# State-space decay without selecting products: exponents loaded onto all partitions, all differences by ScalarE; the residual's loads two pieces ahead

## The chip, the core and the metric

The kernel runs on one core of a Trainium2 chip. The metric is the device time of one execution in microseconds (us), from the first to the last instruction with what lies around them; lower is better. The core has TensorE (PE: matrix products, with PEld for its weight loads), VectorE (DVE), ScalarE (ACT), GpSimd (POOL) and SyncE (SP, which here only issues transfers). The engines run their own instruction streams in order and wait for each other through semaphores. PSUM is the memory into which TensorE writes; SBUF holds the operands.

## The reference

One inference step of a one-layer decoder: attention over a sliding window beside a state-space mixer (Mamba-2 SSD), whose outputs are concatenated, projected (`w_out`) and added to the residual, then a squared-ReLU MLP. There are 1040 prompt tokens (16 meta tokens and 1024) and 32 sample tokens (8 sequences of 4). What matters here is the chunked scan: 8 heads of 64, 2 groups, a state of 128, chunks of 128 tokens.

```python
def ssd_scan(x, dt, a, bm, cm, h0, chunk):
    ...
    xdt = (x * dt[..., None]).reshape(b, nc, chunk, H, P)
    acum = jnp.cumsum((dt * a).reshape(b, nc, chunk, H), axis=2)
    causal = jnp.tril(jnp.ones((chunk, chunk), dtype=bool))[None, None, :, :, None]
    seg = acum[:, :, :, None, :] - acum[:, :, None, :, :]
    decay = jnp.exp(jnp.where(causal, seg, -jnp.inf))
    g = jnp.einsum('bcthn,bcshn->bctsh', ch, bh) * decay
    y_diag = jnp.einsum('bctsh,bcshp->bcthp', g, xdt)
    to_end = jnp.exp(acum[:, :, -1:, :] - acum)
    s_chunk = jnp.einsum('bclhn,bclh,bclhp->bchpn', bh, to_end, xdt)
    total = jnp.exp(acum[:, :, -1, :])
    ...
    y_off = jnp.einsum('bclhn,bchpn->bclhp', ch, h_in) * jnp.exp(acum)[..., None]
    return (y_diag + y_off).reshape(b, L, H, P), h_final
```

`decay` is the object of the change: for each head a matrix of exp(acum[t] - acum[s]) for s up to t. So is exp(acum[t]), the factor of `y_off`.

## The kernel before

Tokens lie along the free dimension and features along the partitions, in 9 token tiles: tile 0 holds the 32 sample tokens and the 16 meta tokens (48), tiles 1 to 8 hold 128 each. Products with weights run in three token chunks of 304 or 288, 384 and 384 columns, and each value is split in two parts (`hi`, `lo`), so that a product is three matmuls per block of 128 features (`gemm`).

The work goes through these parts: the input projections with the attention and the convolution between them (`projections`, up to about 291 us of the profile), then `wout_stream`, then the MLP from about 448 us on.

`wout_stream` goes over the output projection twice. First 24 pieces (8 row blocks times 3 chunks) with the attention half of `w_out`: for each piece it loads the residual `hb` from `xm`, runs a `gemm` of 12 matmuls into a PSUM tile `g`, adds `g` to `hb` on VectorE (L1007) and stores `hb` to `hd` in device memory (L1008). Then, once the state-space output is there, pieces with the other half (`mixer_half`), which read `hd` back into `ha` and store to `he`.

Between the first 24 pieces `interleave` weaves the chains of the state-space tiles: a chain is a Python generator, a slot is one piece with one step of each live chain before it, and a chain starts at its slot. This sets the order in which the program is written down; the planner of the tile framework then sorts each engine's stream by its own costs and due times and lets a transfer move ahead of others where its buffer is free, so the order on SP and on the engines is near the program's, not equal to it. In the trace the first three residual loads stand on SP ahead of the first store of a piece. A tile with a tag and `bufs=n` has n buffers, and the instruction that first writes the n+1st waits until the oldest is no longer read.

The decay before the change. At about 108 us `steps` has the cumulated sums `acum` per token (partition) and head, and writes `A4` with 32 columns per tile: the sum split in two parts (`Ah` and the rest), and the same negated. In the later stage `exponents` (called for tile 0, and for tiles 1 to 4 and 5 to 8 together) turns `A4` by a transpose into a PSUM tile and builds three operands: `L` (one side of the difference, per tile 32 rows), `R` (the other side, times a 0/1 pattern `delta` that picks the head) and `Tr` (the exponents in rows, for `selr`, a 0/1 pattern loaded from the constants). In `ssd(i)`, one product of `L` and `R` per group of four heads gives acum[t] - acum[s] for 4 heads at once in a PSUM tile `pd`; ScalarE takes Relu of the negated difference (L1085) and Exp of its negative (L1086) into `Mt`, and VectorE multiplies by `Gm`, the masked product of B and C (L1087). Four products of `selr` and `Tr` put acum[t] of the right heads onto the right partitions (`pe`), and ScalarE's Exp (L1092) makes `eA` of them.

The rest of `ssd(i)` is not touched: transposes of X and B into `px` and `pb` (L1060, L1062), `xd`, `xw`, `Bt`, `Gm`, the products `y` with `Mt`, the state `hn` and its product `f`, the products with `eA` (L1119) and the sums into X (L1122), then `gate(i)`. Tile 0 goes on with `sample_state` for the states of the sample sequences, which are loaded, scaled (L1183), added to and stored. PSUM tiles with the tag `s` have 3 buffers; `px`, `pb`, the two `pd`, `pe` and others share them.

## Time and profile before

| | |
|---|---|
| median of 3 runs | 1121.79 us (1121.38 to 1121.83) |
| the profiled execution | 1122.73 us |
| its span, first to last instruction | 1120.9 us |
| granted clock of TensorE | 0.999 of full speed |
| instructions | 21721 |

The profile is of one execution. Busy times are given per engine; a matmul's end is modelled and matmuls overlap, so a busy TensorE is not one at its peak, and the distance from one start to the next tells more than a duration. A row of the timeline is start, duration, engine, line and operation, output and inputs, shapes, and how many such instructions stand in it. A row of the waits is engine and line, what it waited for, microseconds in total, times, and the longest. Lines (L1085) are those of the kernel before. Most matmuls have the line of a helper, L205, and are told apart by their tiles.

### The profile page before, as it was taken

What the parts mean: (1) busy time and instruction counts of PE and PEld (TensorE: products, weight loads), DVE (VectorE), ACT (ScalarE), POOL (GpSimd) and SP (SyncE); (2) the same over time, 40 slices, a digit from 0 to 9 for tenths busy, and PEclk for the clock granted to TensorE, in tenths of its full rate; (3) what the DMA queues carried; (4) which work ended last, traced back from release to release, by engine and by line L of the source; (5) the groups of instructions that cost most, each with busy time, mean ns of one, the idle gap of its engine ahead of it and who ended that gap; (6) DMA issues with size and microseconds to landing.
All of it is one profiled execution on the core that took longest, in us unless ns stands there. A gap on an engine that the chain in (4) does not pass through costs nothing.

```text
span 1120.9 us, 21721 instructions
## 1 busy us (share of the span) xinstructions
PE 1105.1 (99%) x8347; PEld 1066.6 (95%) x8347; DVE 834.2 (74%) x1652; ACT 563.9 (50%) x1205; POOL 215.8 (19%) x298
## 2 busy tenths in 40 slices
PE   8999999999999999999999999999999999999997
PEld 8989988988888899999999999999999999999997
DVE  6646888985788968998877777676598657767483
ACT  7312467575766658754444444444434343546461
POOL 0442365564254431200000000000000000000001
PEclk9999999999999999999999999999999999999999
DMA  8231110111575486567643524425989663465273
GB/s 280 77 98 39 39 38 20 39 58 55 183 210 179 136 289 215 199 204 228 195 154 140 177 106 157 161 102 204 393 289 304 191 181 90 134 189 164 77 229 110
DMA packets 84423, 177.56 MB, mean 158 GB/s; under 512 B 10692, under 2 KB 32740, under 8 KB 82272
## 3 DMA queue, kind: packets, MB, share of 16 engines
q1 hardware_dynamic: 77392, 141.52, 40.6%
q0 software_dynamic: 6224, 33.74, 7.5%
q8 instruction: 65, 1.06, 0.4%
q10 hardware_dynamic: 704, 0.92, 0.2%
q14 instruction: 38, 0.31, 0.1%
HBM read 125.42 MB, written 50.72 MB: 157 GB/s over the span
## 4 chain that ended last, share of the span: by engine, by line
PE 77%; DVE 10%; ACT 5%; DMA 4%; issue 2%; POOL 2%; POOLq 0%; SPq 0%; ACTq 0%; DVEq 0%
PE g L205 42%; PE b L205 18%; PE c L205 9%; PE s L205 3%; DMA wdr<-in_wd 2%; PE o L205 1%; DVE bc L527 1%; DMA wraw<-in_win 1%; PE y L205 1%; POOL wlo L237 1%; DVE ts L1637 1%; DVE Sd L1623 1%; PE pt L205 1%; DVE p L680 1%; PE f L205 1%
## 5 line engine op out<-in xcount | busy, mean ns | idle before, releaser
L205 PE MATMUL g<-acth,whi 128*128 128x384 f32 (+2 forms) x528 | 161.8, 331 | 0.2 <-DVE qT L457 0.2
L205 PE MATMUL g<-acth,wlo 128*128 128x384 f32 (+2 forms) x528 | 159.2, 326 | 0.2 <-DVE hb L1007 0.2
L205 PE MATMUL g<-actl,whi 128*128 128x384 f32 (+2 forms) x432 | 140.5, 325 | 0.0
L1636 ACT CAST ts<-tr 128x528 fp32r<-128x528 f32 x92 | 58.2, 632 | 121.4 <-PE b L205 101.9
L1637 DVE TENSOR_TENSOR ts<-tr,ts 128x528 fp32r<-128x528 f32 x92 | 65.1, 708 | 57.5 <-ACT ts L1636 56.0
L205 PEld LDWEIGHTS g<-acth,whi 128*128 128x128 f32 x528 | 97.3, 188 | 2.0 <-issue 1.0
L205 PEld LDWEIGHTS g<-acth,wlo 128*128 128x128 f32 x528 | 97.1, 188 | 0.6 <-DVE hb L1007 0.4
L205 PEld LDWEIGHTS g<-actl,whi 128*128 128x128 f32 x432 | 81.4, 188 | 0.1
L324 POOL TENSOR_TENSOR rs<-rs,nhalf 128x3 f32<-128x3 f32 x9 | 10.3, 1150 | 336.5 <-DMA wdq<-in_wd 286.9
L1352 ACT COPY s<-g 128x264 f32<-128x264 f32 x90 | 33.8, 377 | 61.9 <-PE g L205 61.3
L237 POOL TENSOR_TENSOR wlo<-wraw,whi 128x256 fp32r<-128x256 f32 x56 | 48.9, 904 | 10.9 <-ACT whi L234 10.6
L1425 POOL DMA_DIRECT2D u<-u x16 | 8.5, 532 | 176.3 <-ACT u L1368 146.7
L1357 DVE TENSOR_TENSOR u<-b,s 128x264 f32<-128x264 f32 x64 | 27.5, 430 | 19.5 <-PE b L205 10.1
L1362 ACT ACTIVATE u<-u 128x528 f32<-128x528 f32 x42 | 27.1, 646 | 26.8 <-DVE u L1361 26.8
L205 PE MATMUL b<-ts,w7y 128*128 128x264 f32 x279 | 39.3, 285 | 0.0
L205 PE MATMUL g<-ts,whi 128*128 128x264 f32 x279 | 38.9, 284 | 0.0
L205 PE MATMUL g<-ts,w7y 128*128 128x264 f32 x279 | 38.9, 283 | 0.0
L205 PE MATMUL b<-ts,whi 128*128 128x264 f32 x279 | 38.9, 284 | 0.0
L205 PE MATMUL g<-ts,wlo 128*128 128x264 f32 x270 | 38.0, 285 | 0.0
L205 PE MATMUL b<-ts,wlo 128*128 128x264 f32 x270 | 37.3, 282 | 0.0
L205 PEld LDWEIGHTS b<-ts,w7y 128*128 128x128 f32 x279 | 36.1, 188 | 0.0
L205 PEld LDWEIGHTS b<-ts,whi 128*128 128x128 f32 x279 | 36.0, 188 | 0.0
(590 smaller groups left out, 3445.9 us busy)
## 6 DMA issues: line engine op xcount, KB each, us to landing
tr<-u SPq DMA_DIRECT2D x92, 264.0 KB, 2.8
wraw<-in_wu SPq DMA_DIRECT2D x38, 512.0 KB, 3.9
wdr<-in_wd SPq DMA_DIRECT2D x68, 256.0 KB, 3.7
u<-t POOLq DMA_DIRECT2D x16, 1056.0 KB, 5.7
wraw<-in_win SPq DMA_DIRECT2D x16, 512.0 KB, 3.7
u<-u POOLq DMA_DIRECT2D x10, 792.0 KB, 3.6
wraw<-in_wo SPq DMA_DIRECT2D x24, 256.0 KB, 3.0
h<-he SPq DMA_DIRECT2D x16, 264.0 KB, 5.2
```

The lines of the kernel that those rows point to most:

```text
L205: PE.matmul(out, lhsT=a, rhs=b, start=start, stop=stop, skip_group_check=on)
L237: eng.tensor_tensor(out=lo[:, n], in0=raw[:, n], in1=f(hi[:, n]), op=ALU.subtract)
L324: POOL.tensor_tensor(out=out, in0=out, in1=nhalf[:out.shape[0], :w], op=ALU.pow)
L527: DVE.scalar_tensor_tensor(out=acc, in0=cb[:, j:j + CL], scalar=cw_(j), in1=acc, op0=ALU.mult, op1=ALU.add)
L680: DVE.tensor_tensor_reduce(out=s_out[:, 0:W], in0=ps, in1=mask, scale=-scale, scalar=nsink, op0=ALU.add, op1=ALU.min, accum_out=nm)
L1352: ACT.copy(out=s[:, c], in_=ps[c][:, :TQ])
L1357: DVE.tensor_tensor(out=out[:, c], in0=ps[c][:, :TQ], in1=s[:, c], op=ALU.add)
L1362: ACT.activation(out=x, in_=x, func=AF.Square)
L1425: POOL.dma_start(out=u7[p][:, 4 + a:7], in_=u[:, a:3])
L1623: tt(out=s, in0=s, in1=r, op=ALU.subtract)
L1636: ACT.copy(out=t[:, 0], in_=x)
L1637: DVE.tensor_tensor(out=t[:, 1], in0=x, in1=f(t[:, 0]), op=ALU.subtract)
```

## The change

- `steps` no longer builds `A4` and `Ah`. It keeps `Ac`, the cumulated sums, for all tiles (with a memset of tile 0's part), transposes it once to 72 rows (tile and head) by 128 tokens, and stores two small arrays to device memory: `ad`, the negated sums, and `ed`, their exponentials.
- `exponents`, `L`, `R`, `Tr`, `selr` and the constants `delta`, `mm` and `sel` are gone, and with them the products into `pd` and `pe`.
- `decays(i)`, now for each tile by itself and two slots ahead of `ssd(i)`, loads `Ab`: the 8 rows of the tile out of `ad`, the same on all partitions (128 times 4 KB), and `eA`: for each half of the partitions the rows of four heads out of `ed` (64 times four rows of 512 bytes, twice). Both have two buffers.
- `ssd(i)` makes the differences by ScalarE: for each head a Relu of `Ab` with `Ac`'s column as the bias, into `Mt`; then one Exp over all eight heads and one product with `Gm`.
- `wout_stream` loads the residual two pieces ahead, from four buffers instead of three; its first slot only loads, and all chains start one slot later, the chain of tile 0 with its first step one piece earlier against the pieces.

```diff
@@ steps
-        Ah = pa.tile([128, NT, 8], F32R, name="Ah")
-        Ac = pa.tile([128, NT, 8], F32, name="Ac")
+        POOL.memset(Ac[:, 0], 0.0)
         for rows, s in ((128, slice(1, NT)), (48, slice(0, 1))):
             DVE.tensor_copy(out=Ac[:rows, s], in_=acum[:rows, s])
-            ACT.copy(out=Ah[:rows, s], in_=acum[:rows, s])
...
-            DVE.tensor_copy(out=A4[:rows, s, 0:8], in_=f(Ah[:rows, s]))
-            DVE.tensor_tensor(out=A4[:rows, s, 8:16], in0=Ac[:rows, s], in1=f(Ah[:rows, s]), op=ALU.subtract)
-            DVE.tensor_scalar(out=A4[:rows, s, 16:32], in0=A4[:rows, s, 0:16], scalar1=-1.0, scalar2=None, op0=ALU.mult)
+        yield
+
+        tp = ps_tile("o")
+        PE.transpose(tp[:F9, 0:128], Ac.rearrange("p i h -> p (i h)"), ident)
+        for n, (dst, func, sign) in enumerate(((ad, AF.Copy, -1.0), (ed, AF.Exp, 1.0))):
+            t = pa.tile([F9, 128], F32, name=f"At{n}")
+            ACT.activation(out=t, in_=tp[:F9, 0:128], func=func, scale=sign)
+            SP.dma_start(out=dst, in_=t)
@@ in place of exponents
-    selr = sp.tile([128, 4, 128], F32R, name="selr")
...
-    def exponents(rows, w, s):
...
+    def decays(i):
+
+        M = TOK[i][1]
+        z = "0" if i == 0 else ""
+        Ab = sp.tile([128, 8, M], F32, name="Ab", tag="Ab" + z, bufs=1 if i == 0 else 2)
+        SP.dma_start(out=Ab[:M], in_=ad[8 * i:8 * i + 8, 0:M].unsqueeze(0).broadcast_to([M, 8, M]))
+        eA = sp.tile([128, 4, M], F32, name="eA", tag="eA" + z, bufs=1 if i == 0 else 2)
+        for hh in range(2):
+            src = ed[8 * i:8 * i + 8, 0:M].rearrange("(j q) t -> q j t", q=2)[hh]
+            SP.dma_start(out=eA[HALF[hh]], in_=src.unsqueeze(0).broadcast_to([64, 4, M]))
+        DEC[i] = Ab, eA
+        yield
@@ wout_stream
-        for m, ch in [(0, 0), (0, 1), (1, 0), (1, 1), (0, 2), (1, 2)] + [(m, ch) for m in range(2, 8) for ch in range(3)]:
+        order = [(0, 0), (0, 1), (1, 0), (1, 1), (0, 2), (1, 2)] + [(m, ch) for m in range(2, 8) for ch in range(3)]
+
+        def load_x(m, ch):
+            c0, cw = CM[ch]
+            hb = sp.tile([128, 384], F32, name="hb", tag="hb", bufs=4)[:, :cw]
+            SP.dma_start(out=hb, in_=xm[:, 8 * c0 + m * cw:8 * c0 + (m + 1) * cw])
+            hbs.append(hb)
+
+        load_x(*order[0])
+        load_x(*order[1])
+        yield
+        for n, (m, ch) in enumerate(order):
...
-            hb = sp.tile([128, 384], F32, name="hb", tag="hb", bufs=3)[:, :cw]
-            SP.dma_start(out=hb, in_=xm[:, 8 * c0 + m * cw:8 * c0 + (m + 1) * cw])
+            if n + 2 < len(order):
+                load_x(*order[n + 2])
+            hb = hbs.pop(0)
@@ ssd
-        for g in range(2):
-            pd = ptile()
-            mm(pd[:M, :4 * M], L[:, :M], R[:, 4 * g:4 * g + 4, :M], True, True)
-
-            mt = Mt[:M, g, :, :M]
-            ACT.activation(out=mt, in_=pd[:M, :4 * M].rearrange("p (r t) -> p r t", r=4), func=AF.Relu, scale=-1.0)
-            ACT.activation(out=mt, in_=mt, func=AF.Exp, scale=-1.0)
-            DVE.tensor_tensor(out=mt, in0=mt, in1=Gm[:M, g, :M].unsqueeze(1).broadcast_to([M, 4, M]), op=ALU.mult)
-        eA = sp.tile([128, 4, M], F32, name="eA", tag="eA" + z, bufs=nb)
-        pe = ptile()
-        for j in range(4):
-            mm(pe[:, j * M:j * M + M], sl[:, j, :], Tr[:, :M], True, True)
-        ACT.activation(out=eA, in_=pe[:, :4 * M].rearrange("p (j t) -> p j t", j=4), func=AF.Exp)
+        mt = Mt[:M, :, :, :M]
+        for h in range(8):
+            e, a = Mt[:M, h // 4, h % 4, :M], Ac[:M, i, h:h + 1]
+            ACT.activation(out=e, in_=Ab[:M, h], func=AF.Relu, bias=a)
+        ACT.activation(out=mt, in_=mt, func=AF.Exp, scale=-1.0)
+        DVE.tensor_tensor(out=mt, in0=mt, in1=Gm[:M, :, :M].unsqueeze(2).broadcast_to([M, 2, 4, M]), op=ALU.mult)
@@ order of the chains
-    def mixer(i):
-        if i == 0:
-            yield from decays(i)
-        yield from ssd(i)
-
-    interleave(wout_stream(), [(12 if i == 5 else round(2.25 * i), mixer(i)) for i in range(NT)] +
-               [(1, decays(1)), (10, decays(5))])
+    def at_slot(i):
+        return 1 + (12 if i == 5 else round(2.25 * i))
+
+    interleave(wout_stream(), [(max(1, at_slot(i) - 2), decays(i)) for i in range(NT)] +
+               [(at_slot(i), ssd(i)) for i in range(NT)])
```

More of the change, by code (lines that the diff above doesn't have):

```diff
@@ L357, in body @@
     ex = xp.tile([128, NT, 8], F32, name="ex")
-    A4 = xp.tile([128, NT, 32], F32, name="A4")
+    Ac = xp.tile([128, NT, 8], F32, name="Ac")
+    ad = dram.tile([NT * 8, 128], F32, name="ad")
+    ed = dram.tile([NT * 8, 128], F32, name="ed")
     X = act_tiles(CH)
@@ L927, in body @@
     ppt = w3.enter_context(pool("ppt", space=PSUM))
-    selr = sp.tile([128, 4, 128], F32R, name="selr")
-    a, b = CCOL["sel"]
-    POOL.dma_start(out=selr.rearrange("p j q -> p (j q)"), in_=consts[:, a:b])
-    mmc = c("mm")
-    LR = {}
-    def exponents(rows, w, s):
-        n = w // 32
-        tp = ptile()
-        PE.transpose(tp[:w, :rows], A4[:rows, s, :], ident[:rows, :rows])
-        if n > 1:
-            L = sp.tile([128, 4, 128], F32R, name="L", tag="L", bufs=1)
-            Tr = sp.tile([128, 4, 128], F32R, name="Tr", tag="Tr", bufs=1)
-            R = sp.tile([128, 8, 128], F32R, name="R", tag="R", bufs=1)
-            POOL.memset(f(L), 0.0)
-            POOL.memset(f(Tr), 0.0)
-        else:
-            L = sp.tile([128, 1, T0], F32R, name="L0")
-            Tr = sp.tile([128, 1, T0], F32R, name="Tr0")
-            R = sp.tile([128, 8, 128], F32R, name="R0", tag="Bm", bufs=1)
-        tm = sp.tile([128, 128], F32, name="tm", tag="dg", bufs=2)
-        DVE.tensor_scalar(out=tm[:w, :rows], in0=tp[:w, :rows], scalar1=mmc[:w, 1:2], scalar2=mmc[:w, 0:1], op0=ALU.mult, op1=ALU.add)
-        for h in range(0, 8, 4):
-            DVE.tensor_tensor(out=R[:w, h:h + 4, :rows], in0=tm[:w, :rows].unsqueeze(1).broadcast_to([w, 4, rows]),
-                              in1=c("delta", w)[:, h:h + 4].unsqueeze(2).broadcast_to([w, 4, rows]), op=ALU.mult)
-        for q in range(n):
-            rr = slice(32 * q, 32 * q + 32)
-            DVE.tensor_scalar(out=L[rr, q, :rows], in0=tp[rr, :rows], scalar1=mmc[rr, 0:1], scalar2=mmc[rr, 1:2],
-                              op0=ALU.mult, op1=ALU.add)
-            ACT.copy(out=Tr[rr, q, :rows], in_=tp[rr, :rows])
-        for q, i in enumerate(range(s.start, s.stop)):
-            LR[i] = (L[:w, q], R[:w], Tr[:w, q], selr[:w])
@@ new lines, in body @@
+    DEC = {}
+    def decays(i):
[9 more added lines that the diff above has]
+        yield
```

26 lines of the change are left out of this document (3 added, 23 removed).

## The prediction

> **What bounds the kernel now.** I read the page's engine totals first, then the stage in which the change works by windows, the stage behind it, and the chain of waits across both.
>
> ```profile
> span 1120.9 us, 21721 instructions
> ...
> PE 1105.1 (99%) x8347; PEld 1066.6 (95%) x8347; DVE 834.2 (74%) x1652; ACT 563.9 (50%) x1205; POOL 215.8 (19%) x298
> ```
>
> TensorE is busy for 99% of the span, so a change pays only where it shortens TensorE's own stream or a wait in it. The stage is the first half of the output projection with the state-space tiles between its pieces, 291 to 398 us. The columns are the stretch and its length, busy time (and count) of PE, PEld, DVE, ACT and POOL, the granted clock, the DMA share and GB/s:
>
> ```profile
> 291.00:310.00 19.00, 18.25 (x132) 14.98 (x133) 16.94 (x36) 14.65 (x41) 7.19 (x12) 1.00 0.84 256
> 310.00:330.00 20.00, 19.94 (x164) 17.65 (x163) 17.38 (x32) 13.53 (x35) 9.09 (x10) 1.00 0.69 204
> 330.00:350.00 20.00, 19.30 (x153) 16.90 (x152) 17.95 (x40) 10.79 (x29) 10.10 (x10) 1.00 0.71 222
> 350.00:370.00 20.00, 19.39 (x146) 16.07 (x144) 16.72 (x40) 13.86 (x36) 8.28 (x9) 1.00 0.44 133
> 370.00:390.00 20.00, 19.63 (x141) 17.49 (x141) 18.20 (x41) 13.63 (x33) 8.24 (x9) 1.00 0.44 138
> 390.00:398.00 8.00, 8.00 (x56) 7.77 (x54) 6.75 (x20) 2.01 (x5) 4.09 (x5) 1.00 0.55 179
> sum 107.00, PE 104.51 PEld 90.85 DVE 93.93 ACT 68.47 POOL 46.98; mean PE 17.42 PEld 15.14 DVE 15.66 ACT 11.41 POOL 7.83
> ```
>
> In 107 us TensorE is without a matmul for 2.5 us (107 - 104.51) and without a weight load for 16.15 us (107 - 90.85). VectorE has 13 us left, ScalarE 38.5, GpSimd 60. The DMA engines are used at 0.84 down to 0.44: weighted by the lengths, 66.0 us of full use, 44.0 of it in the first 59 us.
>
> The stage behind it shows what a gain is worth once it is won:
>
> ```profile
> 398.00:410.00 12.00, 12.00 (x83) 12.00 (x82) 6.55 (x18) 5.87 (x12) 5.73 (x6) 1.00 0.95 330
> 410.00:420.00 10.00, 10.00 (x68) 10.00 (x67) 6.51 (x13) 6.03 (x11) 1.33 (x2) 1.00 0.88 307
> ```
>
> There TensorE and its weight loads fill every microsecond, so a stage that ends earlier should move all of what follows. The chain from 285 to 410 us says who sets the pace inside the stage:
>
> ```profile
> by line: PE g L205 33.1%; PE s L205 15.3%; PE y L205 7.1%; PE f L205 4.6%; issue 4.3%; ACT Mt L1085 2.7%; ACT Mt L1086 2.6%; ACT st L1183 2.0%; DVE L L956 1.8%; DVE actl L550 1.8%; DVE Mt L1087 1.6%; DVE xs L1122 1.5%; DVE hb L1007 1.5%; PE
> ```
>
> About 60% of it is matmuls (g, s, y, f); the rest goes through VectorE and ScalarE in pieces of 2% or 3%, four of which the change removes or rewrites (the three Mt lines and L956). So TensorE is the nearest bound, and the decay chain is one of the things that hold it up.
>
> **The change, part by part.** *Matmuls removed.* A tile of 128 loses two 512-column matmuls for the differences and four 128-column ones for the broadcast exponents. Starts one after the other:
>
> ```profile
> 311.18 0.71 PE L205 MATMUL s<-R,L 128*128 128x512 f32 x2
> 311.72 0.56 PE L205 MATMUL s<-Tr,selr 128*128 128x128 f32 x4
> 312.12 0.39 PE L205 MATMUL g<-acth,wlo 128*128 128x384 f32 x1
> ```
>
> 0.54 us for the pair (311.72 - 311.18) and 0.40 for the four (312.12 - 311.72), 0.94 a tile, 7.5 for eight. I go by starts, as matmuls overlap. Tile 0 has the same six in smaller shapes; I put 0.7 for it (between 0.4 and 0.94, by the larger, since a narrow matmul still loads weights), and 0.3 for the three transposes of the exponents (estimates from the four at 0.10 each). Sum removed on PE: 8.5 us, on the path nearly all the time.
>
> *The step chain,* around 108 us, loses the copies of A4 and Ah and gains a memset on GpSimd, one transpose, two activations and two small stores on SP:
>
> ```profile
> 104.00:116.00 12.00, 12.00 (x80) 11.53 (x80) 6.07 (x21) 5.25 (x18) 3.18 (x6) 1.00 0.07 26
> ```
>
> ```profile
> 111.79 1.42 PE o L205 x10
> ```
>
> TensorE is full there and covers the rest (VectorE, ScalarE and GpSimd have half or more of the time free), so the transpose costs its 0.1 us and a wait for its one-buffered bank o; bounds 0 and 1.4 us, one use of that bank in the chain. I take 0.2, near the lower end: nothing is queued for it but two stores.
>
> *Waits removed.* Three of eight PSUM tiles per state tile go, and with them the trip from TensorE to ScalarE and back:
>
> ```profile
> ACT Mt L1085 <- PE s L205: 6.7, 4, 2.6
> ...
> PEld s L1060 <- ACT Tr L958: 0.9, 1, 0.9
> ...
> PEld s L1062 <- ACT eA L1092: 0.9, 2, 0.4
> ...
> PEld s L1060 <- ACT Mt L1086: 0.7, 3, 0.3
> ...
> PEld s L205 <- ACT eA L1092: 0.6, 2, 0.4
> PEld s L205 <- ACT Mt L1085: 0.6, 2, 0.3
> ```
>
> The five PEld rows, 3.7 us together, are TensorE standing at a PSUM tile that ScalarE still reads or at the exponents. Between 0 and 3.7 comes back. Since TensorE was without a matmul for only 2.5 us in all, I take 1.2. ScalarE's 6.7 us behind TensorE goes too, but ScalarE has room and I count it at nothing; its 38.5 idle us cover it.
>
> *VectorE.*
>
> ```profile
> L956 DVE TENSOR_SCALAR L<-s,cs 32x128 fp32r<-32x128 f32 x8 | 3.2, 405 | 0.7 <-ACT Tr L958 0.5
> ...
> L205 PEld LDWEIGHTS s<-R,L 128*128 128x128 f32 x16 | 2.8, 190 | 0.4 <-ACT Tr L958 0.2
> ...
> L952 DVE TENSOR_TENSOR R<-tm,cs 128x512 fp32r<-128x512 f32 x4 | 2.5, 671 | 0.0
> ...
> L958 ACT CAST Tr<-s 32x128 fp32r<-32x128 f32 x8 | 2.0, 255 | 3.3 <-DVE L L956 3.2
> ```
>
> Gone are R (four of 0.67, two smaller at half), L (eight of 0.4, one smaller) and three tm of about L's size: some 8 us busy. The product with Gm becomes one instruction per tile instead of two:
>
> ```profile
> 314.48 1.29 DVE L1087 TENSOR_TENSOR Mt<-Mt,Gm 128x512 f32<-128x512 f32 x2
> ```
>
> Two take 1.29 us in a row, so one of twice the width costs 1.2 (two bodies, one start) and 0.1 a tile is saved, at the price that the y matmuls get both halves at the end instead of one earlier. VectorE falls from 93.9 to about 85 of a shorter stage. It stays second; no further gain is booked.
>
> *ScalarE.* Per tile it had the following, and now has eight Relus of 128x128 with the bias from a column and one Exp of 1024:
>
> ```profile
> 303.43 1.17 ACT L1085 ACTIVATE Mt<-s 128x512 f32<-128x512 f32 x2
> 304.49 1.14 ACT L1086 ACTIVATE Mt<-Mt 128x512 f32<-128x512 f32 x2
> 305.53 0.59 ACT L1092 ACTIVATE eA<-s 128x512 f32<-128x512 f32 x1
> 306.00 0.59 ACT L1112 COPY hn<-s 128x512 f32<-128x512 f32 x1
> ...
> 318.37 2.45 ACT L1183 ACTIVATE st<-st,e 128x128 f32<-128x128 f32 x8 [1.88 <-DVE e L1181]
> ```
>
> Before: 1.06 + 1.04 + 0.47 = 2.57 us from start to start (303.43, 304.49, 305.53, 306.00). After: the nearest row for the eight Relus is the last one, eight 128x128 activations with a scale from a column, 2.45 us; the Exp costs about 1.05. That is 3.5, so +0.9 a tile, +7.5 for eight and the small one, less nine casts of Tr (0.255 each, 2.3): +5.2 us on an engine with 38.5 free. ScalarE runs in order, and what stands behind the block of 3.5 us (Bt, the weight casts, the state scaling) waits up to 0.9 us longer per tile, with GpSimd and TensorE behind these. Bounds 0 and 8 us; I take 0.8, near the lower end, because the Relus no longer wait for TensorE and can run as soon as their load is in.
>
> [...]
>
> *Loads.* Each tile now reads 512 KB onto all partitions (Ab) and 256 KB in rows of 512 bytes (eA, two issues); tile 0 less, but in pieces of 192 bytes. That is 6.5 MB more in this stage, less the 256 KB of selr:
>
> ```profile
> q1 hardware_dynamic: 15000, 19.98, 60.3%
> ...
> st<-in_st SPq DMA_DIRECT2D x4, 512.0 KB, 4.8
> ...
> zt<-zd SPq DMA_DIRECT2D x8, 256.0 KB, 3.3
> ```
>
> SP's queue moved 19.98 MB from 291 to 400 in 65.7 us of full use (0.603 of 109), so 3.3 us per MB: 21 us more, by the mean. The nearest rows are the state loads (same size as Ab, landing 4.8) and zt (same form as eA, landing 3.3). Lower end 19 us (330 GB/s at a share of 0.95 from 398 to 410 is 347 at full use); upper end 41, all that the stage left free (107 - 66.0), since no row shows a load that reads one 4 KB place 128 times. I take 21, by the two nearest rows, which have the packets' sizes. Then 66.0 + 21 - 0.9 (selr, 0.26 MB) = 86 us of DMA in a stage of 100: full, not over. In the first half it is 44.0 + 14 (five tiles and the small one) in some 55 us, which is over, so loads there land later. What hides it: Ab and eA are asked for two slots (some 9 us at 107/24 a slot) ahead, the residual two pieces. Bounds 0 and 5 us of stall; I take 1.5.
>
> [...]
>
> *Queues.* 27 issues more stand on SP, three per tile. By the nearest rows, a state load and a zt, that is 0.38 + 2 x 0.59 a tile, 14 us of a queue that stands still much of the time:
>
> ```profile
> 297.81 0.38 SPq L1146 DMA_DIRECT2D sT<-in_sT  x1
> 298.25 0.59 SPq L1196 DMA_DIRECT2D zt<-zd  x1
> ```
>
> ```profile
> SPq L1004 <- DMA hd<-hb: 17.9, 13, 3.0
> ```
>
> An Ab waits for the last Relu of the tile two back, an eA for that tile's last product; for tiles 7 and 8 the load is asked for one slot before that product. Behind it stand the residual's loads and stores and the weights. The residual is now asked for two pieces ahead from four buffers instead of three, which takes away most of the 17.9 us of waiting at its load. VectorE itself hardly felt that load:
>
> ```profile
> DVE hb L1007 <- DMA hb<-in_xm: 0.3, 1, 0.3
> ```
>
> so the earlier residual is worth 0.3 at most and I book nothing for it; it pays for the 27 issues. GpSimd loses four memsets and the selr load; it had 60 us idle, nothing is booked. State tile 0 starts one piece earlier against the projection; the tiles behind keep their place.
>
> **Sum.** -8.5 - 1.2 + 0.2 + 0.8 + 1.5 = -7.2 us. The profiled execution took 1122.73 us (span 1120.9), 0.94 above the median of 1121.79. So 1115.5 beside the profiled one, and 1114.6 for a median run.
>
> **The rivals.**
> *ScalarE takes the place (still faster).* If the block of 3.5 us is on the path in every tile, 5.2 of the gain go back in place of 0.8: -2.8 us, 1119.0. For it: both Mt lines of ScalarE stand in the chain with 2.7% and 2.6%, and the product now waits for both halves. Against: 38.5 us idle.
>
> *TensorE has slack and the alternation of VectorE and ScalarE sets the pace (no change).* Weight loads are idle for 16 us, far more than matmuls. Then the removed matmuls free nothing; VectorE gives 8, ScalarE takes 5.2, one wait of Ab takes 1: -1.8 us, 1120.0. Against: the 512-column matmul occupies TensorE 0.27 us, longer than its weight load of 0.19, so idle weight loads are no proof of slack; and the stage behind has both full. [...]
>
> *The DMA engines become the bound (slower).* Place: the first half, 291 to 350. If reading one place 128 times goes at half the mean rate, Ab and eA cost 42 us instead of 21, DMA needs 66.0 + 42 - 0.9 = 107 us, as long as the stage was, and the first half 44 + 28 = 72 of 59 us; part slides into the second half, which is at 0.44. I put the stage 5 us above before: 1127. It decides from 41 us of added use on. For it: 0.84 already at the start, and no row for such a load. Against: packets of the same sizes at other addresses go at 3.3 us per MB.
>
> **Chances.** Forecast 0.60 (own range 1110 to 1118), ScalarE 0.13, slack 0.11, DMA 0.16. Within 0.2% (2.2 us, about what a measurement of this kernel can tell from no change) lies the slack rival. So faster 0.73, same 0.11, slower 0.16. The low end takes all waits back and no new ones: -8.5 - 3.7 = -12.2, 1109.6; the high end holds the slack rival and the milder part of the DMA one, 1123.
>
> **What would show it.** Matmuls into s fewer by 54 and transposes by three; the stage some 100 us long with TensorE's idle time not above 4 us; the Relu line at 8 x 0.3 us per tile and waiting on a load only in the first tiles; DMA share near 0.9, highest from 291 to 330; the waits of PEld on ScalarE lines gone; in the stage behind, the same rows as before, 7 us earlier. Wrong it would be if Ab lands after 9 us or more, if TensorE's idle time in the stage grows past 10 us, or if SP stands at an eA load while the residual waits.

## Result, and the profile after

The changed kernel takes 1126.99 us, median of four runs (1126.49 to 1128.37), against 1121.81 (1121.38 to 1123.36) for the kernel before on the same chip: ratio 1.0047, 95% interval 1.0035 to 1.0059. It is slower by 5.2 us; the prediction was 1114.6 us and faster, so it was wrong in sign, and the time lies outside its range. The profiled execution took 1128.37 us, 5.64 above the profiled one of before. The page of the changed kernel, span and totals:

```profile
span 1126.6 us, 21630 instructions
...
PE 1100.9 (98%) x8291; PEld 1065.2 (95%) x8291; DVE 828.1 (74%) x1619; ACT 568.8 (50%) x1232; POOL 217.7 (19%) x294
```

TensorE has 56 instructions fewer (the 57 that were to go, less the new transpose), and it is busy 4.2 us less in a span 5.7 us longer. The windows of the stage and of the stage behind it, in the stretches shown of before:

```profile
291.00:310.00 19.00, 18.72 (x144) 17.17 (x145) 12.07 (x24) 16.68 (x50) 6.45 (x8) 1.00 0.88 244
310.00:330.00 20.00, 18.95 (x154) 16.24 (x152) 15.27 (x31) 12.54 (x36) 10.12 (x8) 1.00 0.81 241
330.00:350.00 20.00, 17.14 (x135) 15.03 (x135) 18.04 (x37) 13.60 (x40) 5.96 (x6) 1.00 1.04 339
350.00:370.00 20.00, 18.18 (x127) 15.61 (x125) 15.98 (x32) 15.18 (x45) 9.06 (x8) 0.83 0.63 198
370.00:390.00 20.00, 18.51 (x140) 16.55 (x140) 19.32 (x37) 10.60 (x27) 10.10 (x8) 1.00 0.65 194
390.00:398.00 8.00, 7.16 (x43) 6.54 (x41) 7.51 (x22) 4.04 (x8) 6.11 (x6) 1.00 0.78 224
sum 107.00, PE 98.65 PEld 87.13 DVE 88.20 ACT 72.63 POOL 47.78; mean PE 16.44 PEld 14.52 DVE 14.70 ACT 12.11 POOL 7.96
```

```profile
398.00:410.00 12.00, 10.38 (x66) 10.06 (x66) 6.25 (x18) 4.60 (x10) 6.61 (x7) 1.00 1.02 378
410.00:420.00 10.00, 6.12 (x25) 5.89 (x26) 3.97 (x6) 6.17 (x10) 1.84 (x3) 0.66 0.61 203
```

TensorE is without a matmul for 8.35 us of the 107, where it was 2.5, and then for 5.5 of the 22 behind, where it was none. In two stretches the granted clock, 1.00 all through before, is 0.83 and 0.66. The stage did not get shorter: the last of the 24 residual additions starts at 398.55 us (before 397.95). The last addition into ha ends at 454.83 us (before 449.23), and from there on the two programs run 5.6 us apart.

The two longest waits of TensorE, from its timeline (start, duration, then in brackets the idle time ahead and what ended it):

```profile
360.33 0.42 PE L188 MATMUL s<-ones,sqy 128*128 128x1 f32 x2 [1.82 <-DVE sqy L356]
...
413.88 0.61 PE L188 MATMUL g<-acth,wlo 128*128 128x288 f32 x1 [4.64 <-ACT wlo L229]
```

The second is for weights of the second half of the projection. SyncE's timeline shows where their load stood, behind the five loads of ha:

```profile
400.09 3.27 SPq L1001 DMA_DIRECT2D ha<-hd  x5
403.40 0.65 SPq L226 DMA_DIRECT2D wraw<-in_wo  x1
```

It is issued at 403.40 and lands 9.79 us later, where the median of these loads from 291 to 400 us is 3.5 us; in the row of 398 to 410 the DMA engines are at 1.02. In SyncE's program of before 13 weight loads stand ahead of those of ha, in the changed one 11.

Behind both gaps TensorE is full and slow. Windows of 5 us:

```profile
355.00:360.00 5.00, 3.51 (x30) 2.89 (x28) 4.87 (x11) 2.67 (x7) 2.20 (x1) 1.00 0.76 262
360.00:365.00 5.00, 4.67 (x15) 3.63 (x16) 2.56 (x8) 3.39 (x9) 2.00 (x3) 0.55 0.29 89
365.00:370.00 5.00, 5.00 (x34) 4.48 (x32) 4.42 (x7) 4.98 (x18) 1.89 (x2) 0.77 0.69 212
410.00:415.00 5.00, 1.12 (x3) 0.89 (x4) 0.69 (x1) 1.81 (x4) 1.84 (x3) 0.67 0.78 293
415.00:420.00 5.00, 5.00 (x23) 5.00 (x23) 3.28 (x5) 4.35 (x7) 0.00 (x0) 0.65 0.44 113
```

From 415 to 420 TensorE is busy for all 5 us and gets 23 matmuls done, at a clock of 0.65, where 34 fit at full speed (68 in 10 us from 410 to 420 before). So each of these two stalls cost its length and some microseconds of slow work behind it, 5.7 us for both. This gives a sum that closes. I take windows of 1 us from 291 us to the end of the last addition into ha; work is PE's busy time times the granted clock, "clock" is busy time times what is missing to 1, idle is the rest:

```
                    length   work    idle   clock (us)
before               158.2   155.5    2.7     0.0
after                163.8   144.3   13.9     5.7
difference            +5.6   -11.2  +11.2    +5.7
```

The work went as the change promises. Idle time took all of it back, and what is left over, the loss, is as large as what the lower clock cost.

The loads, for 291 to 400 us (queue: packets, MB, share; then KB of one and median us to landing):

```profile
q1 hardware_dynamic: 21230, 26.56, 79.7%
...
Ab<-ad SPq DMA_DIRECT2D x8, 512.0 KB, 6.9
hb<-in_xm SPq DMA_DIRECT2D x16, 192.0 KB, 3.9
...
eA<-ed SPq DMA_DIRECT2D x16, 128.0 KB, 4.9
```

6.58 MB more cost 21.1 us more of full use (0.797 and 0.603 of 109), which is the 21 that was taken; the residual's pieces land in 3.9 us (192 KB) where it was 3.0. The decay's own instructions, by form, and one product with what GpSimd does beside it:

```profile
L1064 ACT ACTIVATE Mt<-Ab,Ac 128x128 f32<-128x128 f32 x64 | 20.0, 390 | 0.5 <-DMA Ab<-ad 0.5
...
L1066 DVE TENSOR_TENSOR Mt<-Mt,Gm 128x1024 f32<-128x1024 f32 x8 | 14.4, 1797 | 1.1 <-ACT Mt L1065 1.0
...
L1065 ACT ACTIVATE Mt<-Mt 128x1024 f32<-128x1024 f32 x8 | 8.4, 1054 | 0.1
```

```profile
327.40 1.94 POOL L1129 TENSOR_TENSOR Bm<-BS,cs 96x1024 fp32r<-96x1024 f32 x1
...
328.40 3.03 DVE L1066 TENSOR_TENSOR Mt<-Mt,Gm 128x1024 f32<-128x1024 f32 x1
```

The product takes 1.8 us in the mean, not 1.2. GpSimd stands beside another VectorE instruction too, in front of the first of the two long waits:

```profile
357.38 2.20 POOL L1181 TENSOR_TENSOR actl<-xs,acth 128x512 fp32r<-128x512 f32 x1 [4.13 <-ACT acth L1180]
...
358.55 1.31 DVE L355 TENSOR_TENSOR sqy<-sqy 128x256 f32<-128x256 f32 x1
```

This addition takes 0.42 us in the three tiles before, and in all eight tiles of the kernel before the change; its stretch is 0.9 of the 1.82 us. Last, the waits from 285 to 410 us and SyncE's from 291 to 400:

```profile
PE y L188 <- DVE Mt L1066: 3.2, 3, 1.5
...
PE s L188 <- DVE sqy L356: 2.9, 3, 1.8
...
PEld s L188 <- ACT Mt L1064: 2.4, 2, 2.1
```

```profile
SPq L928 <- DVE xs L1096: 6.1, 3, 2.6
```

The five rows of weight loads that waited for ScalarE are gone with the instructions that they name; other waits for VectorE and ScalarE have come, one of them again of weight loads (2.4 us), and SyncE now stands at loads of eA until the buffer of the tile two back is free.

### The profile page after: what moved, and what is told of

It is laid out like the page before. It is cut to its first block, busy times and chain, and to the rows that moved or that the text cites. A ratio compares the mean times of both kernels' runs of the same rounds, so it can differ in the third digit from the quotient of the medians.

```text
span 1126.6 us, 21630 instructions
## 1 busy us (share of the span) xinstructions
PE 1100.9 (98%) x8291; PEld 1065.2 (95%) x8291; DVE 828.1 (74%) x1619; ACT 568.8 (50%) x1232; POOL 217.7 (19%) x294
## 4 chain that ended last, share of the span: by engine, by line
PE 81%; DVE 8%; DMA 4%; ACT 3%; POOL 2%; issue 2%; SPq 0%; POOLq 0%; DVEq 0%; ACTq 0%
PE g L188 45%; PE b L188 20%; PE c L188 10%; PE s L188 2%; PE o L188 1%; DMA hd<-hb 1%; DVE bc L512 1%; DMA wraw<-in_win 1%; DMA hb<-in_xm 1%; DMA wraw<-in_wo 1%; POOL wlo L220 1%; PE pt L188 1%; DVE Mt L1066 1%; DVE p L665 1%; ACT acth L395 0%
## 5 line engine op out<-in xcount | busy, mean ns | idle before, releaser
L188 PE MATMUL g<-acth,wlo 128*128 128x384 f32 (+2 forms) x528 | 161.5, 332 | 4.6 <-ACT wlo L229 4.6
L220 POOL TENSOR_TENSOR wlo<-wraw,whi 128x256 fp32r<-128x256 f32 x56 | 49.0, 904 | 11.0 <-ACT whi L217 10.7
L188 PEld LDWEIGHTS g<-ts,w7y 128*128 128x128 f32 x279 | 36.3, 188 | 0.0
```

The costliest lines, as they stand in the source:

```text
L188: PE.matmul(out, lhsT=a, rhs=b, start=start, stop=stop, skip_group_check=on)
L220: eng.tensor_tensor(out=lo[:, n], in0=raw[:, n], in1=f(hi[:, n]), op=ALU.subtract)
```

## The experiments

Two theories at the start. **Theory 1:** the loads of Ab and eA cost; they delay the residual's pieces and push the weight loads back in SyncE's order. **Theory 2:** the product with Gm, 1024 wide and up to 3.03 us long beside GpSimd, costs. Ratios are to the kernel before on the same chip, with 95% intervals; a distance between two kernels is the difference of their ratios, at 1.12 us for 0.001.

**e1, loads for two tiles only.**

```diff
 def decays(i):
+    if i > 1:
+        DEC[i] = DEC[1]; yield; return
```

(The product with eA then goes to a tile of its own, and the decay values of tiles 2 to 8 are left out.)

> The changed kernel, but Ab and eA are loaded for tiles 0 and 1 alone and tiles 2 to 8 use those of tile 1 (their decay values are left out; the instructions on VectorE and ScalarE are as many and as wide). SyncE issues 21 loads less and some 5.5 MB less are moved, 18 us of DMA use by the rate of the stage. Theory 1 (the loads are what costs: they delay the residual's pieces in the stage and push the mixer's weight loads back in SyncE's order until one lands behind the loads of ha): 1116 to 1120 us, no gap of 4.6 us at the weights of m = 3, last residual add before 396 us. Theory 2 (the 1024-wide Gm product that GpSimd stretches is what costs): 1124 to 1127 us, TensorE still idle for 7 us or more in the stage.

1118.77 us, 0.9972 (0.9960 to 0.9983): 8.4 us under the changed kernel. The last residual addition is at 394.01 us, no gap over 1.5 us is left, and no window below full clock. Theory 1 is right so far as that the loads cost; the expected 1116 to 1120 is met.

**e2, the product in two.**

```diff
-        DVE.tensor_tensor(out=mt, in0=mt, in1=Gm[:M, :, :M].unsqueeze(2)..., op=ALU.mult)
+        for g in range(2):
+            DVE.tensor_tensor(out=Mt[:M, g, :, :M], in0=Mt[:M, g, :, :M], in1=Gm[:M, g, :M]..., op=ALU.mult)
```

> The changed kernel with the Gm product as two products 512 wide, as before the change. Theory 2: VectorE's stretched products (15 us for 9) go back to some 11.4 us for 18, the waits of the y product and its weights for Mt go, 1122 to 1124 us. Theory 1: within 1 us of the changed kernel, 1126 to 1128 us, since the same loads stand in the same queue.

1130.90 us, 1.0083 (1.0070 to 1.0096): slower still, which neither theory expected. But the edit did not take the stretch away:

```profile
L1067 DVE TENSOR_TENSOR Mt<-Mt,Gm 128x512 f32<-128x512 f32 x16 | 15.0, 960 | 2.4 <-ACT Mt L1065 2.4
```

That is 15.0 us for the products of tiles 1 to 8, against 14.4 in the changed kernel and 10.7 before, where the expectation had 11.4 for all. So e2 leaves theory 2 open; e13 answers it. TensorE's timeline of this kernel has other gaps in place of those two:

```profile
362.07 0.35 PE L188 MATMUL s<-ones,sqy 128*128 128x1 f32 x2 [2.51 <-DVE sqy L356]
...
400.08 0.49 PE L188 MATMUL s<-dg,ones 128*128 128x128 f32 x2 [2.41 <-ACT dg L364]
...
418.57 0.40 PE L188 MATMUL g<-acth,whi 128*128 128x288 f32 x1 [1.97 <-ACT whi L229]
```

**e4, the loads issued by GpSimd.**

```diff
-        SP.dma_start(out=Ab[:M], ...)      (and the two of eA)
+        POOL.dma_start(out=Ab[:M], ...)
```

> The changed kernel with the loads of Ab and eA issued by GpSimd in place of SyncE: the same bytes on the same 16 engines, SyncE's queue 27 issues shorter, so that nothing of the residual or the weights stands behind an eA load there, and seven weight loads of the mixer from m = 0 to m = 6 stand further ahead of the ha loads in its order. If SyncE's queue and order are what costs: 1118 to 1122 us, with the gap at the weights of m = 3 gone. If the bytes themselves are what costs: 1125 to 1128 us, and the residual's pieces still land 0.9 us later than before the change. [...]

1129.24 us, 1.0076 (1.0063 to 1.0088). The gap at the weights is gone (13 of their loads stand ahead of ha), but the stage has a worse one:

```profile
321.87 1.98 PE L188 MATMUL y<-Mt,xd 128*64 128x128 f32 x16 [5.71 <-DVE Mt L1066]
```

The product stands in VectorE's order behind a multiplication that waits for a load:

```profile
319.90 0.69 DVE L1171 SCALAR_TENSOR_TENSOR xs<-xs,zt 128x512 f32<-128x512 f32 x1 [6.08 <-DMA zt<-zd]
```

This load (zt) was issued at 309.57 us and landed 10.2 us later, where the median was 3.3 before the change. Another wait of TensorE, 3.84 us, stands behind a product that took 6.36 us beside GpSimd. The time lies above the ranges for the queue and for the bytes. GpSimd's issues took 0.6 us each. The run doesn't tell queue from bytes, since GpSimd's work and VectorE's beside it change as well.

**e7, the residual's loads as before the change.**

```diff
-            if n + 2 < len(order):
-                load_x(*order[n + 2])
-            hb = hbs.pop(0)
+            hb = sp.tile([128, 384], F32, name="hb", tag="hb", bufs=3)[:, :cw]
+            SP.dma_start(out=hb, in_=xm[...])
```

(Where the second pass reads hd back, its tile `hb` goes back from four buffers to three as well, here and in e9, e14, e20 and e21.)

> The changed kernel with the residual's pieces loaded as before the change (each load in its own step, 3 buffers). If the loads two ahead cost nothing or hide a little: 1127 to 1129 us. If it is they that move the weight loads back in SyncE's order: 1122 to 1125 us, and the weights of m = 3 land ahead of the ha loads.

1123.24 us, 1.0023 (1.0012 to 1.0034): the loads two ahead, with the fourth buffers, cost 2.7 us beside those of eA, and without them 13 weight loads stand ahead of ha and that gap is gone. The decay's part alone is still slower than before.

**e10, the 21 loads put back, small.**

```diff
 (on e1)
+            SP.dma_start(out=Ar, in_=ad[8 * i:8 * i + 1].broadcast_to([128, 128]))
+            for hh in range(2):
+                SP.dma_start(out=er[HALF[hh]], in_=ed[8 * i:8 * i + 1].broadcast_to([64, 128]))
```

> The kernel of e1 (tiles 2 to 8 use Ab and eA of tile 1, their decay values left out) with 21 small loads put back in the places of the ones taken out: SyncE issues as many loads as the changed kernel, but each of the 21 brings an eighth or a quarter of the bytes (128 x 128 and twice 64 x 128 values a tile, 0.9 MB in all in place of 5.5). If the bytes cost: as e1, 1117 to 1120 us. If the issues in SyncE's queue cost: as the changed kernel, 1125 to 1128 us, with an SP that stands at those loads while the residual's pieces wait, and the mixer's weight loads at the places in its order that they have in the changed kernel.

1122.62 us, 1.0010 (1.0001 to 1.0019), between the two and 4.3 us above e1. The stage ends as in e1 (393.71 us); TensorE's timeline has two gaps, with 3.4 us lost to the clock behind them:

```profile
374.01 1.59 PE L188 MATMUL y<-Mt,xd 128*64 128x128 f32 x16 [2.37 <-DVE Mt L1075]
...
427.64 0.83 PE L188 MATMUL c<-ones,sq 128*128 128x1 f32 x6 [1.47 <-DVE sq L966]
```

**e6, the weight loads issued by ScalarE.**

```diff
-        SP.dma_start(out=raw, in_=wo[m, half])
+        ACT.dma_start(out=raw, in_=wo[m, half])
```

> The changed kernel with the mixer's weight loads issued by ScalarE in place of SyncE, so that they no longer stand behind Ab, eA, the residual's pieces and the ha loads. If the late weights of m = 3 cost what the gap shows (4.6 us idle and some 2 us at a lower granted clock behind it): 1120 to 1122 us, no gap above 2 us between 400 and 420. If the gap is only where time lost before comes to light: 1125 to 1128 us with another wait in that place.

1121.54 us, 1.0009 (0.9997 to 1.0020): 4.3 us come back, no gap is over 1.7 us and no window is below full clock. TensorE is idle as much as in the changed kernel up to the last addition into ha (12.0 us against 13.9), but in pieces of 1.67 us at most, behind which the clock stayed at 1.00.

**e8, eA by ScalarE from Ab.**

```diff
-        for hh in range(2):                 (two loads of eA)
+        for hh in range(0 if i else 2):
...
         ACT.activation(out=mt, in_=mt, func=AF.Exp, scale=-1.0)
+        for hh in range(2 if i else 0):
+            ACT.activation(out=eA[HALF[hh]], in_=Ab.rearrange("p (j q) t -> p q j t", q=2)[HALF[hh], hh], func=AF.Exp, scale=-1.0)
```

> The changed kernel with eA of tiles 1 to 8 worked out by ScalarE, two exponentials 64 x 512 from Ab (scale -1), in place of their 16 loads: 2.1 MB and 16 issues less, ScalarE about 1.1 us a tile busier (9 us in a stage in which it is busy 73 of 108). If what the loads cost goes with their number or bytes: 2 to 5 of the 8 us that e1 gained, 1122 to 1125 us. If ScalarE bounds (a rival of the prediction): 1127 us or more, with waits of the Gm product for the exponential above the 3.9 us of the changed kernel.

1116.36 us, 0.9957 (0.9945 to 0.9970): faster than before, and 10.1 us faster than the changed kernel for 16 loads less; more than expected, and no less than e1 gained (8.4). Its sum of windows from 291 to 398 us, the two behind, and two forms:

```profile
sum 107.00, PE 101.18 PEld 90.07 DVE 89.49 ACT 85.84 POOL 50.07; mean PE 16.86 PEld 15.01 DVE 14.91 ACT 14.31 POOL 8.34
```

```profile
398.00:410.00 12.00, 12.00 (x79) 12.00 (x78) 5.44 (x12) 4.97 (x11) 4.89 (x5) 1.00 0.99 382
410.00:420.00 10.00, 10.00 (x68) 10.00 (x67) 8.97 (x16) 8.82 (x15) 0.00 (x0) 1.00 0.55 178
```

```profile
L1068 DVE TENSOR_TENSOR Mt<-Mt,Gm 128x1024 f32<-128x1024 f32 x8 | 11.0, 1381 | 2.3 <-ACT Mt L1065 2.3
...
L1067 ACT ACTIVATE eA<-Ab 64x512 f32<-64x512 f32 x16 | 10.0, 624 | 0.2
```

ScalarE is 13 us busier in the same 107 us than in the changed kernel, and the kernel is still faster than before; the stage behind is full again. ScalarE is not the bound.

**e9, e8 with the old residual** (both edits above).

> The kernel of e8 with the residual's pieces loaded as before the change. If what e7 and e8 save adds up: 1118 to 1121 us, at or under the kernel before. If the two save the same wait: within 1.5 us of the faster of the two.

1119.93 us, 0.9988 (0.9980 to 0.9997). The time is in the range given for savings that add up, but that range reckoned with a smaller gain of e8. The two together save 6.6 us where e8 alone saves 10.1 and e7 2.7, so they don't add up. Loading two ahead, which costs 2.7 us beside the loads of eA, gains 3.5 without them.

**e12, e8 and e6 together.**

> The kernel of e8 (eA of tiles 1 to 8 by ScalarE) with the mixer's weight loads issued by ScalarE as in e6. e8 has no gap at the weights left, so if the two cures mend the same loss: within 1 us of e8, 1115.5 to 1117.5 us. If SyncE's queue still delays the residual in e8: 1113 to 1115 us.

1121.03 us, 1.0000 (0.9989 to 1.0010): worse than e8, against both expectations. e8 has no gap at the weights to mend, and issuing them from ScalarE makes one behind the stage, of 2.12 us: a load of weights issued at 396.55 us lands 9.0 us later.

**e13, Ab and eA one slot later.**

```diff
-    interleave(wout_stream(), [(max(1, at_slot(i) - 2), decays(i)) ...
+    interleave(wout_stream(), [(max(1, at_slot(i) - 1), decays(i)) ...
```

> The changed kernel with the loads of Ab and eA issued one slot ahead of their tile in place of two: the same bytes and as many issues, but the eA buffer of the tile before the last is free by then, so that SyncE does not stand at an eA load (6.1 us in three waits for the sum of xs and eA in the changed kernel). If that standing is what costs: 1121 to 1124 us, and those waits go. If number and bytes of the loads cost: 1126 to 1129 us.

1126.39 us, 1.0052 (1.0040 to 1.0064), as the changed kernel. SyncE standing at eA, a fault named in the prediction, is not what costs: the row of 6.1 us is down to 1.0. Nor is it the product's stretch, theory 2:

```profile
L1066 DVE TENSOR_TENSOR Mt<-Mt,Gm 128x1024 f32<-128x1024 f32 x8 | 10.7, 1341 | 3.1 <-ACT Mt L1065 3.0
```

The eight products take as long as those before the change, and the kernel is as slow as the changed one. Two gaps again:

```profile
393.54 0.80 PE L188 MATMUL s<-dg,ones 128*128 128x128 f32 x2 [2.70 <-ACT dg L364]
...
412.84 0.40 PE L188 MATMUL g<-acth,whi 128*128 128x288 f32 x1 [1.98 <-ACT whi L229]
```

**e14, eA by ScalarE with its loads kept and unread.**

```diff
 (on e9)
+            for hh in range(2):
+                SP.dma_start(out=er[HALF[hh]], in_=src.unsqueeze(0).broadcast_to([64, 4, M]))
```

> The kernel of e9 (eA by ScalarE, the residual as before the change; 1119.9 us) with the 16 loads of eA put back into a tile that nothing reads: the same bytes and issues as the kernel of e7 (1123.2 us), while no instruction waits for them and they wait for no reader. If issues and bytes cost: 1122.5 to 1124 us, as e7. If it costs that eA lands late or that its buffer comes free late: 1119.5 to 1121 us, as e9.

1127.27 us, 1.0060 (1.0048 to 1.0072), 8.1 us above e9 and outside both ranges: loads that nobody waits for cost more than the ones that are read, in e7. So what counts is neither that eA lands late nor the buffer's reader. SyncE itself stood 5.2 us behind these loads, whose one buffer each has to wait for the load before. TensorE's gaps:

```profile
304.04 0.69 PE L188 MATMUL g<-acth,wlo 128*128 128x384 f32 x1 [1.99 <-DVE hb L982]
...
362.09 0.35 PE L188 MATMUL s<-ones,sqy 128*128 128x1 f32 x2 [2.29 <-DVE sqy L356]
```

**e15, e8 with the load of Ab one slot later** (the edit of e13 on e8).

> The kernel of e8 with the loads of Ab issued one slot ahead of their tile in place of two; all else is the same, and the load has landed in 6 us where a slot is about 4 us long and the tile's first Relu comes some 6 us into it. If a kernel of this stage is moved by the order in which its instructions come to stand, and not by one cost: 1117 to 1121 us, with a TensorE gap of 1.3 us or more in the stage that e8 has not. If only costs count: within 1 us of e8, 1115.5 to 1117.5 us.

1115.54 us, 0.9954 (0.9942 to 0.9966), as e8: the gain isn't the luck of one order. This is the lowest median of the study, though e8 and e16 are not told from it by their intervals; all three are faster than both kernels that were compared.

**e16, e8 with Ab in three loads a tile.**

```diff
-        SP.dma_start(out=Ab[:M], in_=ad[8 * i:8 * i + 8, 0:M]...)
+        for a, b in (((0, 4), (4, 6), (6, 8)) if i else ((0, 8),)):
+            SP.dma_start(out=Ab[:M, a:b], in_=ad[8 * i + a:8 * i + b, 0:M]...)
```

> The kernel of e8 (eA by ScalarE) with Ab of tiles 1 to 8 brought by three loads a tile (4, 2 and 2 heads, the last two as large as an eA load) in place of one: the bytes of e8, but as many issues in SyncE's queue as the changed kernel has. If the number of issues is what the loads of eA cost: 1122 to 1127 us, most of the 10.6 us that e8 gained is lost again, with TensorE gaps of 1.3 us or more in the stage. If the bytes are: 1115.5 to 1118 us, as e8. Half each: 1119 to 1122 us.

1116.84 us, 0.9963 (0.9950 to 0.9976), as e8. About as many issues as in the changed kernel cost 0.7 us: their number alone is not it. The queue in 291 to 400 us:

```profile
q1 hardware_dynamic: 20467, 27.39, 81.8%
```

That is more bytes and more use than the slow kernel has in the same stretch, as the stage behind starts earlier. A DMA share of 0.82 here and of 0.80 in the slow kernel: a high share says nothing by itself.

**e17, e1 with an unread load of all of Ab.**

```diff
+            SP.dma_start(out=Ar, in_=ad[8 * i:8 * i + 8].unsqueeze(0).broadcast_to([128, 8, 128]))
```

> The kernel of e1 (tiles 2 to 8 use Ab and eA of tile 1, their decay values left out) with one load of the full Ab a tile put back, into a tile that nothing reads: 7 issues and 3.7 MB, where e10 put back 21 issues and 0.9 MB and lost 3.9 us. If bytes cost: two thirds of what e1 gained is lost, 1123 to 1126 us. If issues cost: a third of e10's loss, 1119 to 1121 us.

1119.53 us, 0.9978 (0.9966 to 0.9989): 0.7 us above e1. Nor is it the bytes alone.

**e5, the weights asked for four ahead.**

```diff
-    weights = Ahead([... for half in range(2) for m in range(8)], 2)
+    weights = Ahead([... for half in range(2) for m in range(8)], 4)
```

> The changed kernel with the mixer's weights asked for four ahead in place of two, still in SyncE's queue: 7 of their loads come to stand between the stage's other loads and ahead of the first ha load, where the changed kernel has 5, two variants with a gap of 2.0 us at the weights have 6, and all without that gap have 7. If the place in SyncE's order makes the gap behind the stage: no gap at the weights between 405 and 420, and 1120 to 1124 us (4.6 us of idle and 2.3 us at the lower clock less, of which some may come back in other waits). If the weights are late for another reason: 1125 to 1128 us.

1128.49 us, 1.0058 (1.0046 to 1.0071). The gap at the weights is gone, as expected of the order, and nothing is gained, outside both ranges: the loss sits in the stage, whose last residual addition is at 401.81 us.

```profile
363.23 0.35 PE L188 MATMUL s<-ones,sqy 128*128 128x1 f32 x2 [2.46 <-ACT Mt L1064]
...
402.12 0.49 PE L188 MATMUL s<-dg,ones 128*128 128x128 f32 x2 [2.73 <-ACT dg L364]
```

**e3, the residual's part alone on the kernel before** (loads two ahead, 3 buffers, slots one later).

> The kernel before with the residual part of the change alone: its pieces loaded two ahead (in 3 buffers in place of 4, for room) and the slots one later. TensorE has no gap above 1.3 us there to fill: by the prediction within 0.3 us and with 7 weight loads ahead of ha, 1120.5 to 1122.5 us. If loading two ahead harms by itself (the changed kernel is 2.7 us slower with it than without): 1123 to 1125 us.

1121.29 us, 1.0001 (0.9992 to 1.0010): nothing, as predicted for a TensorE without gaps (291 to 400 us, busy 106.51 of 109):

```profile
291.00:400.00 109.00, 106.51 (x796) 92.51 (x795) 95.95 (x210) 69.89 (x179) 48.21 (x51) 1.00 0.59 186
```

**e20, e9 with one unread load a tile.**

```diff
+            SP.dma_start(out=er, in_=ed[8 * i:8 * i + 4, 0:M].unsqueeze(0).broadcast_to([128, 4, M]))
```

> The kernel of e9 (1119.9 us) with one load a tile put back that nothing reads, 128 x 512 values: the bytes of e14's unread loads of eA (2.1 MB) in 8 issues over all partitions in place of 16 over 64 partitions each. If the bytes beside the other traffic cost: as e14, 1125 to 1128 us. If the number or the form of the loads costs: 1119.5 to 1122 us.

1121.19 us, 0.9999 (0.9990 to 1.0009). SyncE stands as long behind the one buffer of these loads (5.5 us) as in e14, so that this standing is not what e14 pays for.

**e21, e14 with its unread loads cut to a quarter.**

```diff
-                SP.dma_start(out=er[HALF[hh]], in_=src.unsqueeze(0).broadcast_to([64, 4, M]))
+                SP.dma_start(out=er[HALF[hh], 0:1], in_=src[0:1].unsqueeze(0).broadcast_to([64, 1, M]))
```

> The kernel of e14 with its 16 unread loads cut to a quarter (64 x 128 values each, 0.5 MB in place of 2.1), as many issues in the same places. If number or form costs: as e14, 1125 to 1128 us. If the bytes cost: 1119.5 to 1122 us. If it is neither, but the order in which the instructions come to stand and the TensorE gaps that it leaves: anywhere between, with gaps of 1.8 us or more and a granted clock below 1 behind them where it is slow, and none where it is fast.

1122.74 us, 1.0014 (1.0003 to 1.0026), with one gap in the profiled run and the clock at 0.66 behind it:

```profile
400.63 0.44 PE L188 MATMUL g<-acth,wlo 128*128 128x384 f32 x1 [3.09 <-DVE hb L956]
```

In front of it VectorE waits 2.9 us for a load of hb out of hd, which landed 6.1 us after its issue. e20 and e21 complete a square over e9: the bytes alone cost 1.2 us, the number of loads (with their form, over 64 partitions each) alone 2.9, both together (e14) 8.1, each to about 1.5 us. Together they cost more than the sum of the parts.

**What the runs say together.** The same sum as above, for the profiled execution of each (the length is from 291 us to the end of the last addition into ha):

```
         length   work    idle   clock    ratio    TensorE gaps of 1.3 us or more
before    158.2   155.5    2.7    0.0              none
e3        158.9   156.4    2.5    0.0    1.0001    none
e16       148.6   143.1    5.5    0.0    0.9963    none
e15       149.6   143.9    5.7    0.0    0.9954    none
e8        151.6   145.5    6.1    0.0    0.9957    none
e1        153.2   145.5    7.7    0.0    0.9972    1.44, 1.49
e20       153.8   145.6    8.1    0.0    0.9999    none
e17       155.5   146.3    9.1    0.0    0.9978    1.31, 1.51
e10       155.9   143.4    9.1    3.4    1.0010    2.37, 1.47
e21       156.5   144.9    9.9    1.7    1.0014    3.09
e9        156.8   144.8   10.3    1.7    0.9988    1.51, 1.90
e7        156.8   145.6    9.5    1.7    1.0023    1.99, 1.55
e12       156.9   145.9    9.4    1.7    1.0000    2.12
e6        156.9   144.9   12.0    0.0    1.0009    1.67, 1.48, 1.48
e13       158.8   143.5   10.7    4.6    1.0052    2.70, 1.98
e5        160.7   145.9   13.2    1.7    1.0058    1.31, 2.46, 2.73
e4        161.8   143.7   14.7    3.5    1.0076    1.61, 5.71, 3.84
e14       162.6   146.4   11.7    4.6    1.0060    1.99, 1.34, 2.29
e2        162.9   145.5   14.3    3.2    1.0083    2.51, 2.41, 1.97
after     163.8   144.3   13.9    5.7    1.0047    1.48, 1.33, 1.82, 4.64
```

In all kernels with the new decay the work is 143 to 146 us, 9 to 12 under before. What is left of that gain at the end of the stretch is decided by idle time and clock alone. A row need not fit its ratio to the microsecond: it is one execution, the ratio a median, and what follows the stretch varies too (671.7 us before, 672.0 in e8, 674.8 in e16).

Three things are shown: the loads of eA turn the gain into a loss (e8 against the changed kernel, e14 against e9); neither their number, nor their bytes, nor a wait for them accounts for it alone (e16, e17, e13, e14, e20, e21); and the time is lost in TensorE's gaps and at the lower clock behind them. The place of the weight loads in SyncE's program goes with one gap: with 11 ahead of ha it is 4.64 us (after), with 12 it is 1.97 and 1.98 us (e2, e13), and in the kernels that issue from SyncE and have 13 none of 1.3 us stands at the weights. But mending it alone gains nothing (e5), and in e12 the weights come late out of ScalarE's queue.

What stays open is the link between the loads and the gaps inside the stage. Of the 18 waits of TensorE of 1.8 us or more, four follow on a transfer that landed 6 to 10 us after its issue (4.64 in the changed kernel, 5.71 in e4, 2.12 in e12, 3.09 in e21). In eight others the chain that ended the wait holds a VectorE instruction that ran beside GpSimd and took 0.6 us or more longer than its form takes without it (1.82 in the changed kernel, and one each in e2, e4, e5, e9, e10, e13 and e14). So theory 2 falls as the whole cause (e13), but VectorE's stretches have a hand in single gaps. Such stretches stand in fast kernels too (a product of 2.06 us in e8), where no long wait follows, and no run takes work off GpSimd to try it. Every edit also changes the order in which the instructions of all engines are written, and the runs don't separate what the transfers do on the chip from what they do to that order. The old order with the new loads wasn't tried.

## Why the prediction was wrong

*Matmuls removed, -8.5:* right, and rather too small. The work, by the sum above, fell by 11.2 us in the profiled run and by 10.0 in e8.

*Waits removed, -1.2:* the five rows are gone, but others have come (3.2, 2.9 and 2.4 us in the rows above). Idle time grew where it was to shrink, by 11.2 us in the changed kernel; even in the best kernels it is 5.5 to 6.1 us, not 2.7. A likely reading is that the removed matmuls had covered the alternation of the engines; no run tests it. The rival of slack in TensorE was right in this: the 11 us of work are not worth 11 us. It read the idle weight loads (16 of 107 us before) as that slack; e8 keeps 6.4 of its 10.0 us in the profiled run, so the trace agrees in part.

*Step chain, +0.2:* right; the transpose takes 0.27 us and 100 to 291 us is unchanged.

*VectorE, -0.1 a tile:* wrong; the product takes 1.8 us instead of 1.2, 4.8 us over eight tiles (1.38 in e8). But it isn't what costs: in e13 the products take 10.7 us together, as before the change, and the kernel is as slow.

*ScalarE, +0.8:* right in its reading. Relus and Exp measure 2.5 (20.0 / 8) and 1.05 us a tile, as estimated, and with 10 us more of ScalarE e8 is faster than before. That rival is out.

*Loads, +1.5:* this is the step that failed. The use was right (21.1 us), Ab lands in 6.9 us, under the 9 that was to be the sign of failure, and the DMA rival's mechanism (reading one place many times is slow) did not happen; that its time of 1127 was met is chance. But the stall was sized from one resource, the DMA engines' use, with 5 us as its upper bound. The loads of eA alone cost 10.1 us (the changed kernel against e8), and not as a wait for the loads: with them TensorE's idle time is 13.9 us and not 6.1, and 5.7 us go to the lower clock. By which steps the loads open these gaps stays open.

*Queues, +0:* failed too. The 27 issues took 18.0 us (eA 11.5, Ab 6.5) instead of 14, and the order of SyncE's program, in which weight loads slid behind those of ha, was not looked at. The 0.3 at most for the residual holds by itself, as e3 finds no change to about 1 us. But it is not a constant: 3.5 gained or 2.7 lost, by what it stands beside.

*The stage behind, "the same rows as before, 7 us earlier":* wrong; 5 of the 5.6 us came to light there, as a wait for weights and slow matmuls. The stage was full before and lost those 5 us as one input came late: the weights landed 9.79 us after their issue.

Of the three signs that were to show it wrong only the last came, SyncE standing at eA, and e13 shows that this one did not cost; idle in the stage is 8.35 us, under the 10.

*No term at all:* the granted clock, 5.7 us, the size of the whole loss. Before, TensorE had no gap of 1.3 us from 90 us to its end and the rows of the stage said 1.00, so nothing there showed what a gap costs.

## What to carry to other kernels

Work taken from a busy engine is worth its time only while no gap opens in that engine; here 11.2 us less of work on a TensorE that was 99% busy went with 11.2 us more of idle time. Look for what the removed work was covering, and list every queue's order around the new loads, the weights of the next stage above all. When a value is derived from another that is loaded anyway, compute it on an engine with room in place of loading it: here 16 exponentials of 0.62 us on ScalarE in place of 16 loads of 128 KB gained 10 us. Judge such a change by work, idle and clock apart; the busy share alone (99% and 98%) hides that TensorE was busy at a lower clock (0.55 to 0.77 in four windows of 5 us).
